# The last down-projection group as a product of seven, its products summed in PSUM banks, and the up projection's second half in blocks of 256 columns

## The chip, the cores and the metric

One core of one Trainium2 chip. The metric is the device time of one execution in microseconds (us). The engines are named as in the profile: PE (TensorE, matmul) and PEld (its weight loads), DVE (VectorE), ACT (ScalarE), POOL (GpSimd) and SP (SyncE, which here only issues DMAs). A letter q behind a name (SPq) is that engine's queue of issued DMAs and waits.

## The reference, cut to what matters

The block is one layer over 512 tokens of width 1024. Everything ahead of the MLP (a gated delta rule, a retention, an output projection and a norm) is left as it is. What the change touches is the end:

```python
hn = rmsnorm(x, n_mlp_pre)                       # x: 512 tokens x 1024
ff = jnp.square(jax.nn.relu(hn @ w_up)) @ w_down # w_up 1024 x 4096, w_down 4096 x 1024
return x + rmsnorm(ff, n_mlp_post)
```

Inputs and outputs are fp32. The kernel splits each fp32 operand into a high part (rounded to fp32r) and a low part (the rest), and makes three matmuls of each product: high by high, high by low, low by high.

## The kernel before

**Groups.** The MLP runs over four groups of 1024 columns of `w_up` (which are 1024 rows of `w_down`). Of each group the up projection comes first, then the down projection of the same 1024 features, which is added into `facc`, the 512 x 1024 sum over groups that stays in SBUF.

**Up projection.** `feature_major` makes the transposed product: for 512 columns (four blocks of 128 features, one PSUM bank of tag `mm` each) it loads four weight tiles of 256 rows x 512 columns; each serves 24 matmuls of 512 tokens. A group has two such halves. `Squares.take` empties a bank: ScalarE makes relu and square into `r`, then `split` makes the high part on ScalarE (a cast) and the low part on VectorE (a subtraction).

**Down projection of groups 0 to 2.** The 1024 features x 512 tokens and the 1024 x 1024 weights are cut into quarters, and seven products of quarters take the place of eight (the scheme of Strassen and Winograd). Each product is 2 x 4 x 3 = 24 matmuls of 128 x 128 by 512 columns, with two weight tiles. Three products use sums of quarters: `first_sums` and `other_sums` make those of the features on VectorE, and `BlockSums` those of the weights: a plain DMA copies a quarter into DRAM scratch (`copy`, line 169, SP's queue), and an accumulating DMA of GpSimd adds another to it (`add_block`, line 135, POOL's queue). Copies and adds are dropped into the stream of weight loads by `pace`, one job for each 8.5 us of planned time. The seven results are combined on ScalarE and VectorE through the SBUF tiles `p1` and `u2` into `facc`.

**Down projection of group 3.** It is made with all eight products, by `row_tiles`: eight weight tiles of 128 rows x 1024 columns are loaded, split and kept in SBUF. Row tiles 0 and 1 (a row tile is 128 tokens) are made together, then row tile 2, then 3; `ff_done` adds each to `facc`, norms it (`add_normed`: square sums on ScalarE, weighting by `wpost` on VectorE, a root with one Newton step, the sum with the residual `x2`), and two DMAs store it.

**Weight tiles.** Every weight tile is loaded into one of four `raw` buffers by SP's queue, in order; ScalarE casts it to the high part (line 148), VectorE subtracts to get the low part (line 149). The split halves go into rings of three (`whi`, `wlo`), or into a kept tile. A `raw` buffer comes free when VectorE has made the low part, and SP's next load waits for that.

**Order.** The order of the instructions on each engine is set by a scheduler at build time from priorities; each engine then works through its own queue strictly in that order.

Of the kernel before, what the change touches and what calls it, by code (L numbers as in the profile page):

```python
# [19 lines left out]
P = 128  # L20
# [43 lines left out]
def hybrid_block_kernel(ctx: ExitStack, tc: tile.TileContext, a: dict, out: bass.AP):  # L64
# [137 lines left out]
    ga_sums = BlockSums(w_in, OFF_GA, OFF_GA + 512, "ga", False)  # L202
    vg_sums = [BlockSums(w_in, OFF_VB + h * 512, OFF_GB + h * 512, f"vg{h}", False) for h in range(4)]
    gb_sums = BlockSums(w_in, OFF_GBR, OFF_GBR + 512, "gb", False)
    down_sums = [BlockSums(w_down[grp * D : (grp + 1) * D, :], 0, 512, f"dn{grp}") for grp in range(3)]
    for sums in [z_sums, ga_sums] + vg_sums + [gb_sums] + down_sums:
        later_adds.extend((*pair, sums) for pair in sums.adds())

# [91 lines left out]
        times(d, "s4", x, True)  # L300
        out(0, 1, d, p1, ALU.add)

    def token_product(quarters):

        pinned = []

        def product(pss, x, ks, wts, first):
            wh, wl = wts
            xh, xl = quarters[x]
            for t in range(2):  # L310
                tt = slice(t * P, (t + 1) * P)
                for kk in range(2):
                    k = 2 * ks + kk
                    lhs, rhs = (xh[:, k, tt], xl[:, k, tt]), (wh[:, kk, :], wl[:, kk, :])
                    tick(1536)
                    for i in range(3):
                        m = nc.tensor.matmul(  # L317
                            pss[t], lhs[i // 2], rhs[i % 2],
                            start=first and k + i == 0, stop=k + i == 5, skip_group_check=not first,
                        )  # L320
# [1353 lines left out]
    with tc.tile_pool(name="pm", bufs=1) as pm:  # L1674
# [49 lines left out]
            nc.vector.scalar_tensor_tensor(v[:, 1:2], ss[:, 1:2], 1.0 / D, v[:, 0:1], ALU.mult, ALU.add)  # L1724
            return root(v[:, 1:2])

        def add_normed(t, parts, w):

            fw = pm.tile([P, D], F32, tag="ym", name="fw", bufs=2)

            def weigh(half):
                nc.vector.tensor_tensor(fw[:, hss[half]], parts[half], w[:, hss[half]], ALU.mult)

            y = norm_halves([(p, weigh) for p in parts])
            for half in range(2):
                x = x2[:, t, hss[half]]
                nc.vector.scalar_tensor_tensor(x, fw[:, hss[half]], y, x, ALU.mult, ALU.add)
            return fw
# [50 lines left out]
        class Squares:  # L1789


            def __init__(self, grp):
                self.r = pm.tile([P, 2, 2, 4, 256], F32, tag="r4", name="r4")
                og = [act.tile([P, 2, 4, 256], F32R, tag="og", name="ffq") for _ in range(2)]
                a2 = act.tile([P, 2, 2, 4, 256], F32R, tag="actT", name="ffq")
                self.a2 = a2
                self.dst = {
                    "11": [og[0][:, 0], og[0][:, 1]],
                    "12": [a2[:, 0, 0], a2[:, 1, 0]],
                    "22": [a2[:, 0, 1], a2[:, 1, 1]],  # L1800
                }
                self.last = grp == 3
                if self.last:
                    self.dst["21"] = [og[1][:, 0], og[1][:, 1]]
                else:
                    s23 = act.tile([P, 2, 2, 4, 256], F32R, tag="actT", name="ffq")
                    s4 = pm.tile([P, 2, 4, 256], F32R, tag="s4", name="ffq")
                    for i, s in enumerate((og[1], s23[:, 0], s23[:, 1], s4)):
                        self.dst[f"s{i + 1}"] = [s[:, 0], s[:, 1]]

            def fs(self, name, f):
                return [w[:, f : f + 2, :] for w in self.dst[name]]
# [1 line left out]
            def take(self, kh, f, ps, th=None):  # L1814
# [4 lines left out]
                elif kh:  # L1819
                    square_relu(  # L1820
                        ps.rearrange("p (h t) -> p h t", h=2), r, [self.a2[:, i, :, f, :] for i in range(2)]
                    )
                else:
                    square_relu(ps.rearrange("p (h t) -> p h t", h=2), r, None)
                    for th in range(2):
                        name = f"{th + 1}1"
                        if name in self.dst:
                            split(r[:, th], [w[:, f, :] for w in self.dst[name]])

            def first_sums(self, f):  # L1830

# [4 lines left out]
                nc.vector.tensor_tensor(r11, r22, r11, ALU.subtract)  # L1836
                self.sums_mark = split(r11, self.fs("s2", f))[0]

            def other_sums(self):

                split(self.r[:, 1, 1], self.dst["s1"])
                split(self.r[:, 0, 1], self.dst["s3"])
                nc.vector.tensor_tensor(self.r[:, 1, 0], self.r[:, 1, 0], self.r[:, 0, 0], ALU.add)
                split(self.r[:, 1, 0], self.dst["s4"])

        def seven_down(grp, x):

            src = w_down[grp * D : (grp + 1) * D, :]
            plain, summed = block_products(src, down_sums[grp], token_product(x))
            p1, u2 = ([pm.tile([P, T], F32, tag="u", name=n, bufs=4) for _ in range(2)] for n in ("p1", "u2"))  # L1850

            def add(th, ch, parts, op=ALU.add, new=False):
                with tc.high_priority(400 if new else 0):
                    for t in range(2):
                        dst = facc[:, 2 * th + t, hss[ch]]
                        if new and not grp:
                            nc.scalar.copy(dst, parts[t])
                        else:
                            nc.vector.tensor_tensor(dst, dst, parts[t], op)
# [9 lines left out]
            plain(a, "12", 1, 0, False)  # L1869
            add(0, 0, a, new=True)  # L1870
            b = bank(psm)
            summed(b, "s2", 2, True)
            with tc.high_priority(400):
                for t in range(2):
                    nc.vector.tensor_tensor(u2[t], p1[t], b[t], ALU.add)
            c = bank(psx)
            summed(c, "s1", 1, True)
            add(1, 1, c, new=True)
            summed(b, "s3", 3, False)
            with tc.high_priority(400):  # L1880
                for t in range(2):
                    nc.vector.tensor_tensor(p1[t], p1[t], b[t], ALU.add)
            add(1, 1, p1, ALU.subtract)
            add(1, 0, p1)
            plain(c, "s4", 1, 512, False)
            add(0, 1, c, new=True)
            add(0, 1, u2, ALU.subtract)

        facc = pm.tile([P, 4, D], F32, tag="facc", name="facc")
        for grp in range(4):  # L1890
            sq = Squares(grp)
            for half in range(2):
                for th in (None,) if grp or half else (1, 0):
                    tt = slice(0, T) if th is None else slice(256 * th, 256 * th + 256)
                    pss = feature_major(w_up, [h[:, :, tt] for h in hn], grp * 1024 + half * 512, 512, 8)
                    for f in range(4):
                        with tc.high_priority(150 * half):
                            sq.take(half, f, pss[f], th)
                            if half and f % 2 and not sq.last:
                                sq.first_sums(f - 1)  # L1900
            if not sq.last:
                sq.other_sums()
            if grp < 3:
                seven_down(grp, sq.dst)
            else:
                wk = four_keeps(act, "actT") + s4_keep()
                for i in range(2):
                    h = pm.tile([P, 8, T], F32R, tag=f"hn{i}", name="keep").rearrange("p k t -> p (k t)")
                    wk += [(h[:, j * 1024 : j * 1024 + 1024], h[:, j * 1024 + 1024 : j * 1024 + 2048]) for j in (0, 2)]
                wk += four_keeps(pm, "r4")[:1]  # L1910

                def ff_tile(kt, t):
                    tt = slice((t % 2) * P, (t % 2 + 1) * P)
                    return [w[:, kt % 4, tt] for w in sq.dst[f"{t // 2 + 1}{kt // 4 + 1}"]]

                def ff_done(t, ps):
                    parts = [facc[:, t, hs] for hs in hss]
                    for half in range(2):
                        nc.vector.tensor_tensor(parts[half], parts[half], ps[half], ALU.add)
                    add_normed(t, parts, wpost)  # L1920
                    for half in range(2):
                        eng = nc.scalar if half else nc.sync
                        eng.dma_start(out[0, t * P : (t + 1) * P, hss[half]], x2[:, t, hss[half]])

                row_tiles(w_down, ff_tile, grp * 8, lambda kt: wk[kt], ff_done, ((0, 1), (2,), (3,)))


# [25 lines left out]
```

## Time and profile before

| | us |
|---|---|
| median of three runs (1340.27 to 1342.88) | 1341.09 |
| the profiled execution | 1340.97 |
| its span, first to last instruction | 1339.2 |
| PE busy in the span | 1323.0 (99%) |
| VectorE busy | 935.8 (70%) |
| ScalarE busy | 637.6 (48%) |
| mean granted clock of TensorE | 0.999 |

The span is from the first to the last instruction; the rest of the execution's time, 1340.97 - 1339.2 = 1.8 us, lies around it. Matmuls are pipelined: a matmul of 512 columns is recorded as 0.39 us, but the next one starts 0.23 us after it, so the busy time of PE does not tell how far PE is from its best; the distance between starts does. In the tables of groups a row reads: line, engine, operation, output <- inputs, shapes and count, then busy time, mean ns of one, and the idle time of the engine just before them with what ended it. In the timeline a row is start, duration, engine, line and operation, and in brackets how long the engine had waited and for whom. Where a row of the timeline merges several instructions (x3), its duration runs from the first one's start to the last one's end.

### The profile page before, as it was taken

Reading aid. Unit: us, or ns where it says so; the run is one execution under the profiler, and the core shown is the slowest. Engines: PE = TensorE matmul, PEld = TensorE weight load, DVE = VectorE, ACT = ScalarE, POOL = GpSimd, SP = SyncE. Lnnn points to the kernel's source line nnn. Section 1 sums busy time; section 2 is a strip of 40 time slices with the busy share of each in tenths; the row PEclk is TensorE's granted clock in tenths of the full one; section 3 lists DMA queues with packets and bytes.
Section 4 is the critical chain, followed back from the end, with each engine's and each line's share of the span. In section 5 each row is a group of like instructions: output and inputs, shape, how many; then the busy total and the mean of one; then the engine's idle time right before and its main releaser. Section 6 shows DMA issues by size and latency. Waiting matters only on the chain.

```text
span 1339.2 us, 17492 instructions
## 1 busy us (share of the span) xinstructions
PE 1323.0 (99%) x6615; PEld 1095.8 (82%) x6615; DVE 935.8 (70%) x1575; ACT 637.6 (48%) x1126; POOL 78.1 (6%) x83
## 2 busy tenths in 40 slices
PE   9999999999999999999999999999999999999997
PEld 7888888887788888888888888878888888888886
DVE  6889867485666577877577776889684755829535
ACT  5783436554534533553443443445264745346441
POOL 2101100000000000100010000000001010000000
PEclk9999999999999999999999999999999999999999
DMA  5336952567775665996394361535629893635421
GB/s 192 131 111 157 206 117 72 119 164 179 199 165 136 141 194 145 270 259 124 110 251 111 113 205 61 169 130 173 220 75 247 216 275 115 190 103 177 128 79 63
DMA packets 105701, 210.57 MB, mean 157 GB/s; under 512 B 6598, under 2 KB 30320, under 8 KB 105104
## 3 DMA queue, kind: packets, MB, share of 16 engines
q1 hardware_dynamic: 88592, 167.27, 39.0%
q0 software_dynamic: 14704, 35.30, 16.3%
q10 hardware_dynamic: 2320, 6.89, 1.4%
q8 instruction: 52, 0.85, 0.3%
q14 instruction: 33, 0.27, 0.1%
HBM read 205.21 MB, written 62.93 MB: 200 GB/s over the span
## 4 chain that ended last, share of the span: by engine, by line
PE 83%; DVE 7%; ACT 5%; DMA 4%; issue 1%; DVEq 0%; ACTq 0%; SPq 0%
PE mm L668 17%; PE mm L317 12%; PE mm L95 11%; PE mm L94 11%; PE mm L93 11%; PE dl L317 8%; PE dl L668 5%; DVE wlo L149 2%; DMA raw<-in_w_in_dram 2%; PE dl L93 1%; PE dl L95 1%; PE dl L94 1%; DMA raw<-sums 1%; PE tr L397 1%; PE tr L677 1%
## 5 line engine op out<-in xcount | busy, mean ns | idle before, releaser
L148 ACT CAST whi<-raw 128x1024 fp32r<-128x1024 f32 x259 | 272.0, 1052 | 414.3 <-PE mm L94 94.6
L149 DVE TENSOR_TENSOR wlo<-raw,whi 128x1024 fp32r<-128x1024 f32 x259 | 315.4, 1221 | 213.7 <-ACT whi L148 212.1
L668 PE MATMUL mm<-actT,whi 128*128 128x512 f32 x448 | 144.3, 403 | 0.0
L317 PE MATMUL mm<-whi,xsum 128*128 128x512 f32 x384 | 120.4, 390 | 0.0
L95 PE MATMUL mm<-hn,wlo 128*128 128x512 f32 (+1 forms) x288 | 105.4, 366 | 0.0
L94 PE MATMUL mm<-hn,whi 128*128 128x512 f32 (+1 forms) x288 | 105.3, 366 | 0.0
L93 PE MATMUL mm<-hn,whi 128*128 128x512 f32 (+1 forms) x288 | 105.3, 366 | 0.0
L668 PEld LDWEIGHTS mm<-actT,whi 128*128 128x128 f32 x448 | 80.5, 188 | 14.9
L668 PE MATMUL mm<-actT,wlo 128*128 128x512 f32 x224 | 87.8, 392 | 0.0
L317 PEld LDWEIGHTS mm<-whi,xsum 128*128 128x128 f32 x384 | 72.0, 188 | 14.8
L317 PE MATMUL mm<-wlo,xsum 128*128 128x512 f32 x192 | 75.1, 391 | 0.4 <-DVE wlo L149 0.4
L668 PE MATMUL mm<-whi,og 128*128 128x512 f32 x192 | 62.5, 397 | 0.0
L95 PEld LDWEIGHTS mm<-hn,wlo 128*128 128x128 f32 x288 | 54.3, 189 | 8.8
L94 PEld LDWEIGHTS mm<-hn,whi 128*128 128x128 f32 x288 | 54.3, 189 | 8.7
L93 PEld LDWEIGHTS mm<-hn,whi 128*128 128x128 f32 x288 | 54.3, 189 | 8.7
L668 PE MATMUL mm<-whi,actT 128*128 128x512 f32 x176 | 60.4, 405 | 1.0 <-DVE qf L906 1.0
L317 PE MATMUL dl<-whi,ffq 128*128 128x512 f32 x192 | 61.1, 389 | 0.0
L317 PE MATMUL dl<-whi,actT 128*128 128x512 f32 x192 | 61.0, 389 | 0.0
L1785 DVE TENSOR_TENSOR ffq<-r,ffq 128x512 fp32r<-128x512 f32 (+2 forms) x51 | 33.7, 676 | 29.1 <-ACT ffq L1785 29.0
L135 POOL DMA_DIRECT2D sums<-in_w_in_dram x28 | 32.6, 1163 | 365.3 <-DMA sums<-in_w_in_dram 365.3
L93 PE MATMUL mm<-actT,whi 128*128 128x512 f32 x128 | 51.5, 403 | 0.0
L95 PE MATMUL mm<-actT,wlo 128*128 128x512 f32 x128 | 50.8, 397 | 0.0
(394 smaller groups left out, 2885.9 us busy)
## 6 DMA issues: line engine op xcount, KB each, us to landing
raw<-in_w_in_dram SPq DMA_DIRECT2D x95, 512.0 KB, 4.8
raw<-sums SPq DMA_DIRECT2D x56, 512.0 KB, 4.1
raw<-in_w_up_dram SPq DMA_DIRECT2D x36, 512.0 KB, 5.3
sums<-in_w_in_dram SPq DMA_DIRECT2D x32, 512.0 KB, 5.5
sums<-in_w_in_dram POOLq DMA_DIRECT2D x28, 512.0 KB, 7.8
raw<-in_w_down_dram SPq DMA_DIRECT2D x26, 512.0 KB, 3.9
sums<-in_w_down_dram SPq DMA_DIRECT2D x24, 512.0 KB, 6.7
sums<-sums POOLq DMA_DIRECT2D x16, 512.0 KB, 7.9
```

What stands on the lines that cost most here:

```text
L93: nc.tensor.matmul(ps, lh, rh, start=first, stop=False)
L94: nc.tensor.matmul(ps, lh, rl, start=False, stop=False)
L95: nc.tensor.matmul(ps, ll, rh, start=False, stop=last)
L135: tc.keep_in_program_order(nc.gpsimd.dma_start(dst, src, accum_op=ALU.add))
L148: nc.scalar.copy(hi[:, :n], raw[:, :n])
L149: nc.vector.tensor_tensor(lo[:, :n], raw[:, :n], hi[:, :n], ALU.subtract)
L317: m = nc.tensor.matmul(pss[t], lhs[i // 2], rhs[i % 2], start=first and k + i == 0, stop=k + i == 5, skip_group_check=not first,)
L397: nc.tensor.transpose(ps, src, ident)
L668: m = tc.keep_in_program_order(nc.tensor.matmul(*args, **kwargs))
L677: tc.keep_in_program_order(nc.tensor.transpose(ps, src, ident if by is None else by))
L1785: return nc.scalar.copy(dst[0], r), nc.vector.tensor_tensor(dst[1], r, dst[0], ALU.subtract)
```

## The change

- The last group is made with seven products too; `down_sums` has a fourth set, so eight more copies and eight more accumulating adds of 512 KB go through the DMA queues.
- The seven results are no longer combined through `p1` and `u2`. Three pairs of PSUM banks (`a`, `b`, `c`) each take several products one after the other without being cleared, and after each product the running sum of a bank is added to or subtracted from the quarter of `facc` that needs it.
- The up projection's second half is made as two blocks of 256 columns, with weight tiles of 512 rows x 256 columns; each block's squares and sums are made as soon as it is there.
- In group 3, row tiles 0 and 1 are finished after five products. The last two products are made row tile by row tile (`token_product(x, (t,))`) with weights that are kept in SBUF: `s3` for row tiles 2 and 3, then `22` for 2 and 3. The class `Finish` takes the place of `ff_done` and norms a row tile half by half; all stores of row tiles 2 and 3 are ordered behind the last add.

```diff
-    down_sums = [BlockSums(w_down[grp * D : (grp + 1) * D, :], 0, 512, f"dn{grp}") for grp in range(3)]
+    down_sums = [BlockSums(w_down[grp * D : (grp + 1) * D, :], 0, 512, f"dn{grp}") for grp in range(4)]
...
-            fw = pm.tile([P, D], F32, tag="ym", name="fw", bufs=2)
+            fw = pm.tile([P, D], F32, tag="ym", name="fw", bufs=4)
...
-            def other_sums(self):
-
-                split(self.r[:, 1, 1], self.dst["s1"])
-                split(self.r[:, 0, 1], self.dst["s3"])
-                nc.vector.tensor_tensor(self.r[:, 1, 0], self.r[:, 1, 0], self.r[:, 0, 0], ALU.add)
-                split(self.r[:, 1, 0], self.dst["s4"])
+            def other_sums(self, f, last):
+
+                r, fs = self.r[:, :, :, f : f + 2, :], lambda name: self.fs(name, f)
+                for name in ("s1", "s4", "s3") if last else ("s1", "s3", "s4"):
+                    if name == "s4":
+                        nc.vector.tensor_tensor(r[:, 1, 0], r[:, 1, 0], r[:, 0, 0], ALU.add)
+                    split(r[:, int(name != "s3"), int(name != "s4")], fs(name))
...
+            a = bank(psx)
             plain(a, "11", 0, 0, True)
-            with tc.high_priority(400):
-                for t in range(2):
-                    nc.scalar.copy(p1[t], a[t])
-            d = bank(psm)
-            summed(d, "22", 4, True)
-            add(1, 0, d, new=True)
...
+            add(0, 0, a, new=True, prio=100)
+            b = bank(psm)
+            plain(b, "12", 1, 0, True)
+            add(0, 0, b, prio=0)
+            c = bank(psm)
+
+            def s1():
+                summed(c, "s1", 1, True)
+                add(1, 1, c, new=True)
+
+            def s2():
+                summed(a, "s2", 2, False)
+                add(0, 1, a, ALU.subtract, new=True)
+
+            def s3():
+                summed(a, "s3", 3, False)
+                add(1, 1, a, ALU.subtract)
+
+            for step in (s1, s2) if grp == 3 else (s2, s1, s3):
+                step()
+            plain(c, "s4", 1, 512, False)
+            add(0, 1, c, prio=0)
+            if grp < 3:
+                summed(a, "22", 4, False)
+                add(1, 0, a, new=True)
+                return
+            for t in range(2):
+                rows = Finish(t)
+                for half in range(2):
+                    rows.half(half)
+                for half in range(2):
+                    rows.store(half)
...
+            rows = [Finish(2 + t) for t in range(2)]
+            for name, half, op in (("s3", 1, ALU.subtract), ("22", 0, ALU.add)):
                 for t in range(2):
+                    for ks in range(2):
+                        token_product(x, (t,))(a, name, ks, ws[name, ks], False)
+                    dst = facc[:, 2 + t, hss[half]]
+                    with tc.high_priority(400):
+                        done = nc.vector.tensor_tensor(dst, dst, a[t], op)
+                    rows[t].half(half)
+            for r in rows:
+                for half in range(2):
+                    with tc.issue_after(done.ins):
+                        r.store(half)
...
+            for th in (None,) if grp else (1, 0):
+                tt = slice(0, T) if th is None else slice(256 * th, 256 * th + 256)
+                pss = feature_major(w_up, [h[:, :, tt] for h in hn], grp * 1024, 512, 8)
+                for f in range(4):
+                    sq.take(0, f, pss[f], th)
+            for f in (0, 2):
+                pss = feature_major(w_up, hn, grp * 1024 + 512 + f * P, 256, 8)
+                with tc.high_priority(150):
+                    for i in range(2):
+                        sq.take(1, f + i, pss[i])
+                    sq.first_sums(f)
+                sq.other_sums(f, grp == 3)
+            seven_down(grp, sq.dst)
```

Two places show what this does to the engines' queues. The first is the very end of VectorE's queue, from the second-last add into `facc` (before: row tile 3's first half; after: row tile 2's last half). `facc<-facc,mm` and `facc<-facc,dl` are adds of a PSUM bank, `fw` is the weighting by the norm's gains, `nh_v` and `nr` are the small steps of the norm's root, and `acc<-fw,nr_y,acc` is the final sum that the store waits for. Before:

```order
L1919 TENSOR_TENSOR facc<-facc,mm 128x512
L1732 TENSOR_TENSOR fw<-facc,post 128x512
L1723 TENSOR_SCALAR nh_v<-nh_s 128x1
L1919 TENSOR_TENSOR facc<-facc,mm 128x512
L1732 TENSOR_TENSOR fw<-facc,post 128x512
L1724 SCALAR_TENSOR_TENSOR nh_v<-nh_s,nh_v 128x1
L412 RECIPROCAL nr_y<-nr_y 128x1
L414 SCALAR_TENSOR_TENSOR nr_t<-nr_y 128x1
L415 TENSOR_TENSOR nr_t<-nr_t,nh_v 128x1
L416 SCALAR_TENSOR_TENSOR nr_y<-nr_t,nr_y 128x1
L1737 SCALAR_TENSOR_TENSOR acc<-fw,nr_y,acc 128x512 x2
```

The same end now, from the last add on (the rows ahead of it are the add of row tile 2 and the start of its root):

```order
L1904 TENSOR_TENSOR facc<-facc,dl 128x512
L414 SCALAR_TENSOR_TENSOR nr_t<-nr_y 128x1
L1924 TENSOR_TENSOR fw<-facc,post 128x512
L415 TENSOR_TENSOR nr_t<-nr_t,nh_v 128x1
L1926 SCALAR_TENSOR_TENSOR nh_v<-nh_s,nh_v 128x1
L416 SCALAR_TENSOR_TENSOR nr_y<-nr_t,nr_y 128x1
L1934 SCALAR_TENSOR_TENSOR acc<-fw,nr_y,acc 128x512
L412 RECIPROCAL nr_y<-nr_y 128x1
L1934 SCALAR_TENSOR_TENSOR acc<-fw,nr_y,acc 128x512
```

Behind these rows stand row tile 3's three small steps and its two final sums. So between the last add and row tile 3's final sums stand now, beside row tile 3's own steps, three small steps and both final sums of row tile 2, which before had been through long before.

The second place is SP's queue from the last group's up projection to the end. Before, from the middle of group 2's products on:

```order
L103 DMA raw<-in_w_down_dram 128x2x512 x2
L197 DMA raw<-sums 128x1024 x6
L103 DMA raw<-in_w_down_dram 128x2x512 x2
L103 DMA raw<-in_w_up_dram 128x2x512 x8
L103 DMA raw<-in_w_down_dram 128x1024 x8
L1923 DMA out_dram<-acc 128x512 x4
```

After, with the last copy of a weight quarter for this group in the first row:

```order
L169 DMA sums<-in_w_down_dram 128x2x512
L103 DMA raw<-in_w_up_dram 128x2x512 x4
L103 DMA raw<-in_w_up_dram 128x4x256 x4
L103 DMA raw<-in_w_down_dram 128x2x512 x4
L197 DMA raw<-sums 128x1024 x4
L103 DMA raw<-in_w_down_dram 128x2x512 x2
L197 DMA raw<-sums 128x1024 x4
L1936 DMA out_dram<-acc 128x512 x4
```

The last group now takes fourteen weight tiles for its down projection instead of eight, eight of them from the sums that GpSimd makes, and the eight copies for these sums stand in SP's queue among the weight loads of groups 1 and 2 (the last of them is the first row here).

More of the change, by code (lines that the diff above doesn't have):

```diff
@@ L1801, in __init__ @@
                 }
[L1802 to L1809, printed above, removed]
+                s23 = act.tile([P, 2, 2, 4, 256], F32R, tag="actT", name="ffq")
+                s4 = pm.tile([P, 2, 4, 256], F32R, tag="s4", name="ffq")
+                for i, s in enumerate((og[1], s23[:, 0], s23[:, 1], s4)):
+                    self.dst[f"s{i + 1}"] = [s[:, 0], s[:, 1]]
             def fs(self, name, f):
@@ L1869, in seven_down @@
[L1869 to L1882, printed above, removed]
@@ L1891, in hybrid_block_kernel @@
             sq = Squares(grp)
[L1892 to L1925, printed above, removed]
```

59 lines of the change are left out of this document (41 added, 18 removed).

## The prediction

> **What bounds the kernel now.** The page's busy times and its chain of waits come first.
>
> ```profile
> PE 1323.0 (99%) x6615; PEld 1095.8 (82%) x6615; DVE 935.8 (70%) x1575; ACT 637.6 (48%) x1126; POOL 78.1 (6%) x83
> PE 83%; DVE 7%; ACT 5%; DMA 4%; issue 1%; DVEq 0%; ACTq 0%; SPq 0%
> ```
>
> PE sets the time. Since a busy PE is not PE at its peak, I read the chain for the last 140 us next, for the distance of the matmuls, and the waits of PEld in the MLP (PE itself has none there):
>
> ```profile
> 1206.29 5.44 PE dl L317 x24
> 1211.72 5.44 PE mm L317 x24
> ...
> 1238.92 5.44 PE dl L317 x24
> ...
> 1288.11 0.41 PE mm L94
> ...
> 1331.44 0.24 PE mm L95
> 1331.70 0.70 DVE facc L1919
> PEld mm L94 <- DVE keep L149: 0.3, 1, 0.3
> PEld dl L317 <- DVE wlo L149: 0.3, 1, 0.3
> PEld mm L93 <- ACT r L1780: 0.2, 1, 0.2
> ```
>
> A product of 24 matmuls takes 5.44 us, 0.227 us each, with the next one right behind it; from 1040 us to the last matmul PEld waits 0.8 us in all. So there is no stall left to win in the MLP: only fewer matmuls, or a shorter tail behind the last of them, can make it faster. The tail is this:
>
> ```profile
> 1331.70 0.69 DVE L1919 TENSOR_TENSOR facc<-facc,mm 128x512 f32<-128x512 f32 x1 [3.75 <-PE mm L95]
> 1332.42 0.69 DVE L1732 TENSOR_TENSOR fw<-facc,post 128x512 f32<-128x512 f32 x1
> 1333.24 0.16 DVE L1724 SCALAR_TENSOR_TENSOR nh_v<-nh_s,nh_v 128x1 f32<-128x1 f32 x1
> 1333.67 0.17 DVE L412 RECIPROCAL nr_y<-nr_y 128x1 f32<-128x1 f32 x1 [0.27 <-ACT nr_y L411]
> 1334.26 0.16 DVE L416 SCALAR_TENSOR_TENSOR nr_y<-nr_t,nr_y 128x1 f32<-128x1 f32 x1
> 1334.45 1.42 DVE L1737 SCALAR_TENSOR_TENSOR acc<-fw,nr_y,acc 128x512 f32<-128x512 f32 x2
> 1335.90 0.34 ACTq L1923 DMA_DIRECT2D out_dram<-acc  x1
> ```
>
> The last matmul ends at 1331.44 + 0.24 = 1331.68, VectorE adds at once (it had waited 3.75 us), and its last sum ends at 1334.45 + 1.42 = 1335.87: 4.2 us. The last store and the end take 1339.2 - 1335.9 = 3.3 us more.
>
> **The matmuls removed.** The last group's eight products become seven: 192 matmuls become 168, at the same shape of 128 x 128 by 512. 24 x 0.227 = **-5.44 us**, all of it on the path, if PE stays as dense.
>
> **Up projection in blocks, sums in PSUM: 0.** A weight tile of 512 x 256 serves 2 blocks x 4 x 3 = 24 matmuls, as one of 256 x 512 does, so PE's work is the same; its rows of 1 KB could land later. The first weight loads of the kernel have that shape:
>
> ```profile
> raw<-in_w_in_dram SPq DMA_DIRECT2D x7, 512.0 KB, 4.6
> raw<-in_w_up_dram SPq DMA_DIRECT2D x8, 512.0 KB, 7.9
> raw<-in_w_down_dram SPq DMA_DIRECT2D x8, 512.0 KB, 3.7
> ```
>
> The first row (20 to 70 us) has 4.6 us to landing in tiles of 256 columns; the second is the 512-column form from 1060 to 1110 us, the third from 1255 to 1300. In the up projection a tile lasts 5.44 us and four `raw` buffers are in turn, so even 7.9 us is covered. If that cover went, each us beyond four tiles' time would be a us of PE. The products' new order leaves each bank one product, 5.44 us, between its end and its next use, as `a` had before; in that time two adds of 0.6 us must come. Groups 1 and 2 lose four VectorE adds (18 to 14) and two ScalarE copies each, which nobody waited for: 0.
>
> **Eight more copies and adds: 0, at a bound.** They are paced behind group 2's, so they fill groups 1 and 2, where the DMA engines have room:
>
> ```profile
> 1000.00:1110.00 110.00, 109.71 (x565) 93.95 (x564) 63.35 (x79) 61.95 (x98) 12.00 (x12) 1.00 0.92 238
> 1110.00:1206.00 96.00, 96.00 (x425) 79.49 (x424) 54.02 (x64) 45.94 (x62) 0.00 (x0) 1.00 0.43 137
> 1206.00:1289.00 83.00, 83.00 (x367) 68.50 (x366) 52.77 (x65) 41.42 (x58) 0.00 (x0) 1.00 0.42 134
> 1230.54 21.78 SPq L103 DMA_DIRECT2D raw<-in_w_up_dram  x8
> sums<-in_w_down_dram SPq DMA_DIRECT2D x6, 512.0 KB, 7.9
> sums<-in_w_down_dram POOLq DMA_DIRECT2D x6, 512.0 KB, 13.1
> ```
>
> (The last two numbers are the DMA share and GB/s; PE's busy time is the third.) From 1000 to 1110 us the same kind of jobs ran at a share of 0.92 and PE lost 0.3 us; the next 180 us stand at 0.43. Sixteen jobs more at 8.5 us each make about 136 us of what 1000 to 1110 already is. The last copy stands in SP's queue just ahead of the last group's up weights, which are issued at 1230.5 us: 7.9 us for the copy and 13.1 for the add give 1252, and the first such sum is loaded for a product that begins at 1288 + 10.9 us.
>
> **The new tail: +2.2 us, the term that I had to choose.** VectorE had been half idle in the last group (23.2 us busy in 42.7, from the first row here); now it has a group's sums, twelve weight tiles and four norms in 38.1 us of matmuls. The distance of its instructions in a full queue comes from rows of group 2 and of row tile 0:
>
> ```profile
> 1289.00:1331.70 42.70, 42.66 (x188) 34.86 (x187) 23.16 (x48) 13.69 (x30) 0.00 (x0) 1.00 0.22 75
> 1241.40 1.89 DVE L1859 TENSOR_TENSOR facc<-facc,p 128x512 f32<-128x512 f32 x3
> 1220.10 2.35 DVE L149 TENSOR_TENSOR wlo<-raw,whi 128x1024 fp32r<-128x1024 f32 x2
> 1310.39 0.15 DVE L1723 TENSOR_SCALAR nh_v<-nh_s 128x1 f32<-128x1 f32 x1
> 1310.46 0.67 DVE L1919 TENSOR_TENSOR facc<-facc,mm 128x512 f32<-128x512 f32 x1
> 1206.34 0.69 DVE L1785 TENSOR_TENSOR ffq<-r,ffq 128x512 fp32r<-128x512 f32 x1 [1.46 <-ACT ffq L1785]
> ```
>
> Three adds of 512 end 1.89 us after the first starts, with 0.68 for the last: 0.60 from start to start. Two weight tiles in 2.35 us: 1.14. The two final sums in 1.42: 0.67 each. A small step lets the next start after 0.07 us if that is independent; in the tail above, where each waits for the last, 0.19; I take 0.13. From the end of the last up matmul, VectorE's queue has 12 weight tiles (13.7 us), 9 sums and halves of features, 14 adds into `facc` and 8 weightings (31 x 0.60 = 18.6), 8 final sums (5.3) and 24 small steps (3.1): **40.7 us**. Ahead of the last add stand 35.5 of these. To that come its waits: before the first sums for ScalarE's squares and casts (1.46 in the row above, at the same place of group 2, and some 0.5 for the second feature block), some 0.1 at each of a dozen dependent pairs, and 0.4 for the kept weights' last landing; I estimate 3.5 us. So it reaches the last add at 39.1, when PE ended at 38.1: **1.0 us late**. From the add to the last sum it needs the 4.2 us of before, and row tile 2's two final sums and three small steps (1.33 + 0.4), of which its 0.5 us of idle time between the rows from 1332.42 to 1333.67 hides some: +1.2. Tail 1.0 + 4.2 + 1.2 = 6.4 us: +2.2.
>
> Its bounds: with no lateness and half of the 1.2 hidden, +0.6. With every instruction at its own recorded duration instead of its distance (31 x 0.69, 12 x 1.22, 8 x 0.71, 24 x 0.16: 45.5 us), 4.8 us more: +7.0. I take the low side, since group 2's rows are this kind of queue.
>
> [...]
>
> **Sum.** 1340.97 - 5.44 + 2.2 = **1337.7 us** for an execution like the profiled one, which lies 0.1 us under the median of 1341.09.
>
> **Rivals.** A *slow queue*: VectorE takes the recorded durations; it reaches the last add some 5.8 us late, partly by making PE wait for a bank or low parts. 1340.97 - 5.44 + 7.0 = 1342.5. For it: these are the durations that the trace records. Against it: the distances above, and group 2, where between the gap at 1206.34 and the next one VectorE ran 25 us on end while PE did not wait:
>
> ```profile
> 1231.93 1.22 DVE L149 TENSOR_TENSOR wlo<-raw,whi 128x1024 fp32r<-128x1024 f32 x1 [0.28 <-ACT whi L148]
> ```
>
> A *short tail*: the norms of row tiles 0 to 2 fall into VectorE's gaps, +0.6: 1336.1. For it: 40.7 us of queue is barely over PE's 38.1. Against it: the order of its queue is fixed, so a late row holds all behind it.
>
> *Late weights* (slower): the copies and adds now run beside the products of groups 1 and 2, which take a tile in 2.72 us. Four buffers cover 4 x 2.72 = 10.9 us from issue to use, and from there each us is one of PE.
>
> ```profile
> DMA to landing us min/median/max: 4.1/7.4/16.2
> ```
>
> From 1000 to 1060 us, under the jobs of groups 1 and 2, the latest tile took 16.2 us: 5.3 us too long if it hit a product. Two such hits make 10.6: 1348.3; it decides from 6.1 us on (1343.8). For it: the same jobs will stand beside twice as many products. Against it: PE lost 0.3 us in all of 1000 to 1110, with a median of 7.4 us to landing.
>
> **Chances.** The forecast 0.57, the short tail 0.12, the slow queue 0.18, late weights 0.13. A measurement of this kernel can tell about 0.2% (2.7 us) from no change: faster is below 1338.4, slower above 1343.8. The forecast's own range is 1336.3 to 1339.3, with about 0.86 of its chance below 1338.4: 0.49. Faster 0.49 + 0.12 = 0.61, within 0.2% 0.08 + 0.18 = 0.26, slower 0.13. The range goes from just under the short tail, 1335.8, to 1342.0, most of the slow queue.
>
> **What would show it.** The last up matmul where it was, near 1288; seven products of 5.44 us behind it, the last ending near 1326.2; VectorE without a gap of note in the last 30 us; its last add about 1 us behind the last matmul and its last sum about 6.4; no new waits of PEld. Wrong would be: PE waiting for `wlo`, `keep` or an add of `facc` in the last group (then the queue is slower than I took it), or matmuls of groups 1 and 2 further apart than 0.227 us (late weights).

## The result, and the profile after

| | before | the change |
|---|---|---|
| median of nine runs (us) | 1341.16 (1338.09 to 1342.88) | **1335.0** (1333.11 to 1337.96) |
| the profiled execution | 1340.97 | 1335.0 |
| its span | 1339.2 | 1333.2 |
| first matmul of the first down-projection product, at | 1042.7 | 1040.8 |
| from there to the end of the span | 296.5 | 292.4 |

The ratio is 0.996, with a 95% interval of 0.995 to 0.9971. The forecast was 1337.7, and the lower end of its range 1335.8.

The page of the change shows the engines' busy times and the chain by engine in the same places as before:

```profile
PE 1317.0 (99%) x6591; PEld 1091.5 (82%) x6591; DVE 949.4 (71%) x1599; ACT 650.7 (49%) x1139; POOL 86.2 (6%) x91
...
PE 83%; DVE 7%; ACT 5%; DMA 4%; issue 2%; DVEq 0%; ACTq 0%
```

PE still sets the time. It has 24 matmul records less, VectorE 24 instructions more, GpSimd the eight adds more. The chain of waits has the same distance for a product of 24 matmuls as before, here in groups 0, 1 and 2 (in the last group it runs through VectorE, so that group is read from PE's rows below):

```profile
1040.96 5.44 PE dl L317 x24
...
1123.63 5.44 PE dl L317 x24
...
1205.23 5.44 PE dl L317 x24
...
1237.87 5.44 PE dl L317 x24
```

PE's waits from 940 us to 1340 us are one for a late weight tile's low part, some 30 us into group 0's products, and one ahead of the MLP:

```profile
PE mm L317 <- DVE wlo L149: 0.8, 1, 0.8
PE tr L397 <- DVE fw L1763: 0.3, 1, 0.3
```

Two stretches of the table of busy time show the last group's seven products, and then the tail (columns as before: length, then PE, PEld, DVE, ACT, POOL, the clock, the DMA share, GB/s):

```profile
1286.80:1324.90 38.10, 38.10 (x169) 31.21 (x167) 36.09 (x61) 21.79 (x36) 0.00 (x0) 1.00 0.43 140
1324.90:1330.30 5.40, 0.01 (x1) 0.00 (x0) 5.05 (x15) 0.99 (x4) 0.00 (x0) 0.90 0.26 97
```

VectorE's share of the last group went from 23.16 us in 42.7 to 36.09 us in 38.1, and PE is busy through all of it. From its first matmul's start to its last one's end the last group's down projection took 1331.68 - 1287.72 = 43.96 us before, and takes 1324.91 - 1286.67 = 38.24 now: 5.7 less. The end itself is read in the timeline, PE's last row first:

```profile
1323.16 1.75 PE L317 MATMUL dl<-keep,ffq 128*128 128x512 f32 x7
```

VectorE's rows, from a full stretch of its queue and from the end:

```profile
1300.82 1.87 DVE L1851 TENSOR_TENSOR facc<-facc,mm 128x512 f32<-128x512 f32 x3
...
1323.03 0.68 DVE L1904 TENSOR_TENSOR facc<-facc,dl 128x512 f32<-128x512 f32 x1
...
1324.99 0.16 DVE L412 RECIPROCAL nr_y<-nr_y 128x1 f32<-128x1 f32 x1 [0.27 <-ACT nr_y L411]
1325.07 0.67 DVE L1904 TENSOR_TENSOR facc<-facc,dl 128x512 f32<-128x512 f32 x1
...
1326.86 0.75 DVE L1934 SCALAR_TENSOR_TENSOR acc<-fw,nr_y,acc 128x512 f32<-128x512 f32 x1
...
1327.60 0.73 DVE L1934 SCALAR_TENSOR_TENSOR acc<-fw,nr_y,acc 128x512 f32<-128x512 f32 x1
...
1328.83 1.41 DVE L1934 SCALAR_TENSOR_TENSOR acc<-fw,nr_y,acc 128x512 f32<-128x512 f32 x2
```

The last matmul ends at 1323.16 + 1.75 = 1324.91. The last add starts at 1325.07, 0.16 us later (before, 0.02). It is row tile 3's; row tile 2's, at 1323.03, stood 2.04 us ahead of it, and of the steps between them one (the reciprocal at 1324.99) waited for ScalarE. Between the last add and the last two sums stand row tile 2's two sums, one each at 1326.86 and 1327.60. The last sum ends at 1328.83 + 1.41 = 1330.24, so 5.17 us after the last add began, where it was 4.17 before. From there to the end of the span it is 1333.2 - 1330.24 = 2.97 us, where it was 3.33. Behind the last matmul everything together takes 8.3 us instead of 7.5: the new tail costs **0.8 us, not 2.2**.

The table shows a second piece that the forecast did not have: the MLP's down-projection products began 1.9 us earlier. Of what lies ahead of them only group 0's up projection is changed, and it takes the same time: from its first matmul to the first product 47.4 us in both (995.3 to 1042.7, and 993.4 to 1040.8). What the earlier start is worth is the subject of some of the runs below.

### The profile page after: what moved, and what is told of

It reads as the page before. It is cut to its first block, busy times and chain, and to the rows that moved or that the text cites. A ratio compares the mean times of both kernels' runs of the same rounds, so it can differ in the third digit from the quotient of the medians.

```text
span 1333.2 us, 17536 instructions
## 1 busy us (share of the span) xinstructions
PE 1317.0 (99%) x6591; PEld 1091.5 (82%) x6591; DVE 949.4 (71%) x1599; ACT 650.7 (49%) x1139; POOL 86.2 (6%) x91
## 4 chain that ended last, share of the span: by engine, by line
PE 83%; DVE 7%; ACT 5%; DMA 4%; issue 2%; DVEq 0%; ACTq 0%
PE mm L668 17%; PE mm L317 14%; PE mm L94 10%; PE mm L93 10%; PE mm L95 10%; PE dl L317 9%; PE dl L668 5%; DVE wlo L149 2%; DMA raw<-sums 2%; PE dl L93 1%; PE dl L95 1%; PE dl L94 1%; PE tr L397 1%; PE tr L677 1%; ACT whi L148 1%
## 5 line engine op out<-in xcount | busy, mean ns | idle before, releaser
L148 ACT CAST whi<-raw 128x1024 fp32r<-128x1024 f32 x269 | 282.8, 1053 | 406.6 <-PE mm L317 84.1
L149 DVE TENSOR_TENSOR wlo<-raw,whi 128x1024 fp32r<-128x1024 f32 x269 | 328.1, 1222 | 211.8 <-ACT whi L148 210.6
L668 PE MATMUL mm<-actT,wlo 128*128 128x512 f32 x224 | 87.8, 392 | 0.0
L317 PE MATMUL dl<-whi,ffq 128*128 128x512 f32 x224 | 71.3, 389 | 0.0
L317 PE MATMUL mm<-whi,ffq 128*128 128x512 f32 x192 | 61.0, 389 | 0.0
L1786 DVE TENSOR_TENSOR ffq<-r,ffq 128x512 fp32r<-128x512 f32 (+1 forms) x64 | 39.1, 621 | 27.0 <-ACT ffq L1786 26.9
```

Of the source, the lines that this page charges most:

```text
L148: nc.scalar.copy(hi[:, :n], raw[:, :n])
L149: nc.vector.tensor_tensor(lo[:, :n], raw[:, :n], hi[:, :n], ALU.subtract)
L317: m = nc.tensor.matmul(pss[t], lhs[i // 2], rhs[i % 2], start=first and k + i == 0, stop=k + i == 5, skip_group_check=not first,)
L668: m = tc.keep_in_program_order(nc.tensor.matmul(*args, **kwargs))
L1786: return nc.scalar.copy(dst[0], r), nc.vector.tensor_tensor(dst[1], r, dst[0], ALU.subtract)
```

## The experiments

All times in us. Where a ratio is given, it is to the kernel before, run on the same chip in the same series, with its 95% interval; the kernel before had medians of 1341.16 there (the change), 1339.98 (`scratch_only`, `old_last`, `no_jobs`, `eight`) and 1341.00 (`after_again`, `pool_fw`, `up_whole`). Three of the rows have one execution only, the profiled one.

| run | median (runs) | ratio to before | first product at | from there to the end | lost in group 0 |
|---|---|---|---|---|---|
| before, first profile | 1341.16 (9) | 1 | 1042.7 | 296.5 | 0.2 |
| `before_again` | 1343.88 (1) | | 1045.2 | 296.9 | 0.7 |
| `scratch_only` | 1340.70 (12) | 1.0002 [0.9992, 1.0011] | 1041.6 | 297.2 | 0.9 |
| `old_last` | 1340.05 (11) | 1.0002 [0.9992, 1.0011] | 1042.3 | 297.6 | 1.3 |
| the change | 1335.00 (9) | 0.996 [0.995, 0.9971] | 1040.8 | 292.4 | 1.1 |
| `after_again` | 1336.93 (11) | 0.9972 [0.996, 0.9984] | 1038.9 | 292.5 | 1.2 |
| `no_jobs` | 1337.22 (9) | 0.9972 [0.9959, 0.9985] | 1039.4 | 292.2 | 0.4 |
| `no_row2` | 1333.96 (1) | | 1040.3 | 291.9 | 1.6 |
| `weigh_twice` | 1336.84 (1) | | 1042.3 | 292.7 | 0.5 |
| `eight` | 1341.16 (12) | 1.0005 [0.9993, 1.0016] | 1043.2 | 297.5 | 1.3 |
| `pool_fw` | 1340.00 (12) | 0.9989 [0.998, 0.9997] | 1039.9 | 297.4 | 2.2 |
| `up_whole` | 1343.26 (10) | 1.0016 [1.0004, 1.0028] | 1041.1 | 300.5 | 2.0 |

The last three columns are of each run's profiled execution. The last one is what the 168 matmuls of group 0's down projection take from the first one's start to the next up projection, beyond 168 x 0.2267 us. Most of it is one wait for a late low part of a weight tile, as in the row of the change's waits above. It is part of the column before it, and it scatters between runs with the same code there (0.2 to 0.9 with the old code), so differences of a few tenths are read without it.

**The scratch alone.** The change takes four more DRAM tiles, which move those allocated after them. This kernel is the one before with four unused tiles:

```diff
+    spare = [dr.tile([P, 4, 512], F32, tag=f"dn3{i}", name="sums", bufs=1) for i in (2, 1, 3, 0)]
```

> The kernel before, with a fourth set of four DRAM scratch tiles set aside and never used. The profiled run of the change was already 1.9 us early when the MLP began, ahead of any edited instruction. If the place of tensors in DRAM does this, this kernel is 1 to 2 us faster than the one before and its first down-projection product starts near 1041 us (before: 1042.9). If that was the scatter of single executions, it is within 0.7 us of the kernel before in the median.

The ratio is 1.0002: where the scratch lies changes nothing that can be measured. Its first product did start early, at 1041.6 as expected of a kernel that gains by this, but the next two runs show that one start says little.

**The change and the kernel before, again.** Both unaltered, for the scatter of what lies ahead of the MLP.

> The change once more, unaltered, to part what it does from the scatter of single executions. From the first down-projection product to the end the profiles show 296.5 us before and 292.4 after (4.1 less, 4.9 without a wait of PE in group 0 that also came in a kernel without the edits); the start of that product has moved between 1039.4 and 1043.2 us in six kernels whose work ahead of it is the same. Theory 'the change is worth what the MLP shows': 4 to 5 us under the kernel before, ratio 0.9963 to 0.997, and 292 to 292.5 us from the first product to the end again. Rival 'the work ahead of the MLP became faster too': ratio 0.9955 or less, and the first product starts below 1041 us again.

> The kernel before once more, for the scatter of single executions: from the first down-projection product to the end 296.4 to 297.3 us again. If the work ahead of the MLP is the same in both kernels, its first product may start anywhere between 1039 and 1043 us; if the change makes that work faster, at 1041.5 or later again.

The view of one line's instructions gives the first product of each; first the change again:

```profile
L317 PE MATMUL dl<-whi,ffq x32: 389/389/389, 1038.9 to 1055.0; 128*128 128x512 f32 x32
```

and the kernel before again:

```profile
L317 PE MATMUL dl<-whi,ffq x28: 389/389/389, 1045.2 to 1059.9; 128*128 128x512 f32 x28
```

The same code as in the first profiles began 2.5 us later in the one case and 1.9 us earlier in the other. Over all twelve executions, with the same work ahead but for the blocks of group 0's up projection, the products began between 1038.9 and 1045.2. From there to the end, the pairs agree with themselves: 296.5, 296.9 (and 297.2 in `scratch_only`) against 292.4 and 292.5. So the change in the MLP is **-4.4 us** by the means 296.9 and 292.45; without what is lost in group 0 it is -4.9 (296.2 or 296.3 in all three against 291.3 in both). The two ratios of whole executions give -5.4 (0.4% of 1341) and -3.8 (0.28%), on either side of it; the second, 0.9972, lies just outside the band that I expected.

The rival's other sign came in both runs (starts below 1041 and above 1041.5), so I looked for the place where the starts part. In all twelve executions PE, VectorE and SP work through the same instructions in the same order up to 970 us, and the largest part of the scatter arises between 325 and 370 us, some 600 us ahead of any edited instruction. The 150 matmuls from the 2001st on take 34.0 to 38.2 us there; from their end to the first product it is 678.4 to 679.9 us in all twelve. PE's busy time in this stretch, in the kernel before again and in the change again, and the waits of the former (the latter has none):

```profile
325.00:370.00 45.00, 42.40 (x182) 33.26 (x180) 22.92 (x31) 23.52 (x45) 2.27 (x2) 1.00 0.69 189
325.00:370.00 45.00, 44.99 (x200) 37.32 (x200) 25.97 (x35) 25.89 (x51) 3.40 (x3) 1.00 0.76 204
PE dl L668 <- ACT vt L1309: 1.4, 2, 1.0
PE mm L668 <- DVE wlo L149: 0.8, 1, 0.8
PE dl L668 <- DVE st L1323: 0.3, 1, 0.3
```

So the early start is not work of the changed part. Why these operands are later in one execution than in another was not tried, and whether the edits can move them from afar stays open: the three starts with the old MLP are 1041.6 to 1045.2, the nine with any edit 1038.9 to 1043.2, and these overlap. Open is also whether the change itself adds some of the loss in group 0.

**The last group with eight products, the rest changed.** Only the last group's down projection goes back to the old code; the sums in PSUM stay in groups 0 to 2, and the blocks of 256 columns in all four.

```diff
-    down_sums = [... for grp in range(4)]
+    down_sums = [... for grp in range(3)]
...
+            if grp < 3:
+                seven_down(grp, sq.dst)
+                continue
...
+            row_tiles(w_down, ff_tile, grp * 8, lambda kt: wk[kt], ff_done, ((0, 1), (2,), (3,)))
```

> The new up-projection blocks and the sums in PSUM in groups 0 to 2, but the last group with eight products, stores and tail as before. Theory 'only the matmuls count': within 0.7 us of the kernel before. Rival 'blocks and PSUM sums win something too' (less VectorE work, fewer waits): 1 to 2.5 us faster than before, and then the last group alone won less than its 5.44 us.

The ratio is 1.0002, and 297.6 less the 1.3 lost in group 0 is 296.3, as before. The PSUM sums and the blocks bring nothing by themselves and cost nothing; the gain is all in the last group's down projection.

**The matmuls given back.** The change, with one product of the last group (`s4`) multiplied twice: 24 matmuls more, and no load, split or add more. Its output holds that product twice.

```diff
+            plain, summed = block_products(src, down_sums[grp], token_product(x, twice=("s4",) if grp == 3 else ()))
...
+                    for i in [0, 1, 2] * (2 if x in twice else 1):
```

> The change with the last group's product s4 multiplied twice from the same weights (24 matmuls more, no load, split or add more; the output is not the reference's). If matmuls set the time and VectorE's queue is not late, it is 5.4 us slower than the change. If VectorE's queue is what ends last in the last group (a lateness of 1 us or more), part of the 5.4 is hidden: 3 to 4.5 us slower.

Without the loss in group 0 it is 296.2 against 291.3: the 24 matmuls give back 4.9 us, between the two bands that I expected. Ahead of the last matmul's end (1330.96 + 1.98 = 1332.94) they take 5.4 us, and the tail behind it is 0.5 shorter, 7.8 instead of 8.3. In VectorE's timeline its add for row tile 2 now waits for PE, and the last add is not late:

```profile
1330.25 0.69 DVE L1904 TENSOR_TENSOR facc<-facc,dl 128x512 f32<-128x512 f32 x1 [0.18 <-PE dl L317]
...
1332.97 0.69 DVE L1904 TENSOR_TENSOR facc<-facc,dl 128x512 f32<-128x512 f32 x1
```

**No copies and adds for the last group.** The sums of weight quarters are replaced by plain quarters, loaded from `w_down`, so the products get weights that are not the sums; the eight copies and eight adds are gone. (A group has four such sums, of two weight tiles each: `s1`, `s2`, `s3` and `22` use them, and `s1` to `s4` use sums of features. That makes five of the seven products, where the text on the kernel before has three.)

```diff
-    down_sums = [... for grp in range(4)]
+    down_sums = [... for grp in range(3)]
...
+    down_sums.append(Unsummed(w_down[3 * D : 4 * D, :]))
```

> The change without the eight copies and eight adds for the last group: its summed weight quarters are replaced by plain ones, so the output is not the reference's. Theory 'the jobs are hidden' (the prediction): same as the change to 0.7 us. Rival 'they cost': the 0.9 us by which group 0's products came later in the change, or more, is won back; 1 to 3 us faster than the change.

292.2 against 292.4; without the loss in group 0 it is 291.8 against 291.3. The copies and adds cost nothing behind group 0, and of group 0's loss at most the 0.7 us by which the two differ. The 0.5 us by which this run is longer lie in its tail of 8.75 us: its last add starts 0.60 us behind the last matmul. In `after_again` it is 0.04, so this distance alone moves by half a us between kernels with the same queue of VectorE. In the change itself, GpSimd issues the last of its adds 60 us before the first product that needs a sum:

```profile
1237.65 1.14 POOL L135 DMA_DIRECT2D sums<-in_w_down_dram  x1 [9.63 <-DMA sums<-in_w_down_dram]
```

**Up projection's second half in one piece.** The change with blocks of 512 columns again; squares and sums are then made of all four blocks after the whole half.

```diff
+            pss = feature_major(w_up, hn, grp * 1024 + 512, 512, 8)
             for f in (0, 2):
-                pss = feature_major(w_up, hn, grp * 1024 + 512 + f * P, 256, 8)
...
-                        sq.take(1, f + i, pss[i])
+                        sq.take(1, f + i, pss[f + i])
```

> The change with the up projection's second half in one piece of 512 columns again. Theory 'the blocks cost nothing and win nothing' (the prediction): same as the change to 0.7 us, no wait of PE. Rival 'the blocks make room for the sums': all four features' sums then come behind the end of the up projection, and in the last group, where s1 is already the third product, PE waits 2 to 5 us for them; groups 1 and 2, with a product more ahead, wait little.

1343.26, slower than before (1.0016), and 300.5 us for the MLP: 8.1 more than the change. PE's waits from 1010 us on, with the low parts of the feature sums (`ffq`) as a new cause:

```profile
PE mm L317 <- DVE ffq L1786: 3.0, 4, 1.5
PE dl L317 <- DVE ffq L1786: 1.5, 3, 0.5
PE dl L317 <- DVE wlo L149: 0.8, 1, 0.8
```

These 4.5 us for `ffq` are the recorded part; PE's weight loads waited 8.0 us for it. By the distances of PE's matmuls from start to start, beyond 0.2267 us each, groups 1 to 3 lose 6.2 us, half of it in the last group, where the change loses nothing. Another 0.9 is lost in group 0, and the tail is 0.7 longer: the last add starts 0.34 us behind the last matmul, and one more final sum stands behind it. So the blocks are worth nothing by themselves, as `old_last` shows, but without them the sums of features come late, in groups 1 and 2 too (1.5 us each), and the new ending does not pay.

**VectorE's load in the last group, more of it.** Row tiles 0 and 1 are weighted twice, four instructions of 512 more, about 2.4 us in the queue.

```diff
+                if self.t < 2:
+                    nc.vector.tensor_tensor(self.fw[:, hs], f, wpost[:, hs], ALU.mult)
```

> The change with the four weightings of row tiles 0 and 1 made twice on VectorE (the same values, the output is the reference's): four more instructions of 0.6 us, 2.4 us in VectorE's queue of the last group. Theory 'VectorE's queue of the last group is just full': its last add, 0.2 us behind the last matmul in the change, falls 1.5 us or more behind, or PE waits in the last two products, and from the first down-projection product to the end it takes 1.5 to 2.5 us more than the change's 292.4. Rival 'VectorE has 2 us to spare there': 292.4 to 292.9 us again.

292.7, or 0.9 us more than the change when both are taken without the loss in group 0 (292.2 against 291.3). In the last 38 us of matmuls VectorE is busy a little longer, and PE waits nowhere:

```profile
1287.80:1325.90 38.10, 38.08 (x169) 31.19 (x167) 36.79 (x63) 21.76 (x35) 0.00 (x0) 1.00 0.38 126
```

The end shows where the rest went:

```profile
1326.21 0.68 DVE L1904 TENSOR_TENSOR facc<-facc,dl 128x512 f32<-128x512 f32 x1
1326.81 0.74 DVE L1936 SCALAR_TENSOR_TENSOR acc<-fw,nr_y,acc 128x512 f32<-128x512 f32 x1
...
1329.23 2.73 DVE L1936 SCALAR_TENSOR_TENSOR acc<-fw,nr_y,acc 128x512 f32<-128x512 f32 x4
```

The last matmul ends at 1325.89, and the last add starts 0.3 us after it instead of 0.16, which is within the 0.04 to 0.60 of the runs above. VectorE's gaps in the stretch shrink from 2.0 to 1.3 us, and one of row tile 1's final sums now stands behind the last add: from there to the last sum's end it takes 5.75 us instead of 5.17, most of the 0.9. Of 2.4 us, about 1.5 found room. The 292.7 taken raw lies in the rival's band of 292.4 to 292.9; without the loss in group 0, a third of the load did cost time. So neither holds as written: the queue had some room, not enough for all of it. It is a single run.

**Row tile 2's final sums left out.** The change without them; what is stored for row tile 2 is the residual alone.

```diff
+                if self.t != 2:
+                    nc.vector.scalar_tensor_tensor(x, self.fw[:, hss[half]], self.y, x, ALU.mult, ALU.add)
-                nc.vector.scalar_tensor_tensor(x, self.fw[:, hss[half]], self.y, x, ALU.mult, ALU.add)
```

> The change without row tile 2's two final sums on VectorE (its rows are stored without the MLP's result, so the output is not the reference's). Theory 'the longer tail is row tile 2's sums standing ahead of row tile 3's': the time from the last add's start to the last sum's end falls from 5.2 us to 4.2. Rival 'VectorE is late because of the whole queue of the last group': it falls by 0.3 us or less, and the last add starts as far behind the last matmul as before.

VectorE's timeline at the end:

```profile
1325.08 0.67 DVE L1904 TENSOR_TENSOR facc<-facc,dl 128x512 f32<-128x512 f32 x1
...
1327.03 0.16 DVE L412 RECIPROCAL nr_y<-nr_y 128x1 f32<-128x1 f32 x1 [0.20 <-ACT nr_y L411]
...
1327.81 1.41 DVE L1935 SCALAR_TENSOR_TENSOR acc<-fw,nr_y,acc 128x512 f32<-128x512 f32 x2
```

From the last add to the last sum's end it takes 1329.22 - 1325.08 = 4.14 us, as before the change (4.17), and the whole MLP without the loss in group 0 is 1.0 shorter, 290.3 against 291.3: the 1.0 us that the change has more in its tail are these two sums. They hide some 0.3 us of their 1.3, since the norm now waits 0.20 us for ScalarE again.

**Weightings on GpSimd.** An attempt to go faster than the change, by taking eight instructions off VectorE.

```diff
-                nc.vector.tensor_tensor(self.fw[:, hs], f, wpost[:, hs], ALU.mult)
+                nc.gpsimd.tensor_tensor(self.fw[:, hs], f, wpost[:, hs], ALU.mult)
```

> The change with the eight weightings (fw) of the last norm on GpSimd instead of VectorE: 8 x 0.6 us less in VectorE's queue, and row tile 2's final sums then stand behind the last add, where VectorE waits for ScalarE. If the tail is VectorE's queue, the time from the last matmul to the last sum falls by 0.5 to 1.0 us. If GpSimd takes over 2 us for one weighting, or slows VectorE, it is the same or up to 2 us longer.

297.4 us, 5 more than the change, 1.1 of it in group 0; by the medians of one series it is 3.1 more (1340.00 against 1336.93). Either is worse than the 2 us that I expected at most. Three of GpSimd's rows, and VectorE's rows beside them:

```profile
1320.80 1.74 POOL L1924 TENSOR_TENSOR fw<-facc,post 128x512 f32<-128x512 f32 x1 [1.95 <-DVE facc L1904]
1324.41 2.98 POOL L1924 TENSOR_TENSOR fw<-facc,post 128x512 f32<-128x512 f32 x2 [1.87 <-DVE facc L1904]
1329.10 1.70 POOL L1924 TENSOR_TENSOR fw<-facc,post 128x512 f32<-128x512 f32 x1 [1.71 <-DVE facc L1904]
```

```profile
1321.64 0.91 DVE L414 SCALAR_TENSOR_TENSOR nr_t<-nr_y 128x1 f32<-128x1 f32 x1
...
1325.25 0.68 DVE L1904 TENSOR_TENSOR facc<-facc,dl 128x512 f32<-128x512 f32 x1
...
1328.94 2.41 DVE L1934 SCALAR_TENSOR_TENSOR acc<-fw,nr_y,acc 128x512 f32<-128x512 f32 x2
```

The last weighting takes 1.70 us there, against 0.69 on VectorE, and VectorE's instructions beside them get longer: two final sums take 2.41 us instead of 1.41, a small step 0.91 instead of 0.15. That step ends at 1321.64 + 0.91 = 1322.55, when GpSimd's ends (1320.80 + 1.74 = 1322.54), so it looks held until then rather than slowed. Not all are: the add at 1325.25, which takes one operand from PSUM, has its usual 0.68, though GpSimd is at work from 1324.41 to 1327.39. Which operands decide was not tried, and by what VectorE is held no run shows. PE's waits there, for banks that VectorE has not added yet, come to 1.7 us.

## Why the prediction was off, by its steps

**The matmuls, -5.44: right.** Products stand 5.44 us apart as before, and `eight` gives 5.4 us back ahead of the last matmul's end. The old last group stood a little wider than 192 x 0.2267 us, so 5.7 went; with the tail's +0.8 this makes the -4.9 that the MLP shows.

**Blocks and sums in PSUM, 0: the sum right, the cover incomplete.** I named only the landing of the weights as what the blocks could touch. `up_whole` shows that the blocks also give VectorE and ScalarE the time for the feature sums; without them the MLP is 8.1 us longer.

**Copies and adds, 0: right.** `no_jobs` has the same MLP within 0.5 us on either reading, and the *late weights* did not come: no wait of PE in groups 1 to 3.

**The tail, +2.2: mis-sized; measured +0.8.** This is the step of the sum that failed. It has three parts.

- *VectorE reaches the last add 1.0 us late*: 0.16 measured, and 0.04 in `after_again`. The distances I took were right: a row of three adds still takes 1.87 us, and 512-column instructions start 0.60 apart. The work was counted a little low: by the order of the queue eight small steps stand behind the last add, so 35.9 us stand ahead of it, not 35.5. What was too high are the 3.5 us of waits, most of which I had estimated without a row. In the 38.10 us VectorE is busy 36.09, so that its gaps are 2.0; with the 0.16 behind the last matmul that makes the 38.3 at which it came to the add, where I had 39.1. I read this as independent work standing next in the queue behind most dependent pairs; no run took that apart. The lateness does not add up to the end either: at row tile 2's last add VectorE is 0.8 us behind PE, but from there to the last add it needs 2.04 us and PE 2.72. An independent instruction starts 0.08 us after a small step, as behind the reciprocal ahead of the last add (1324.99 to 1325.07); I had taken 0.13 as the mean of both kinds.
- *Row tile 2's two sums and small steps, +1.2*: +1.0, shown by `no_row2`.
- *The final store and the end, 3.3 as before*: 2.97. I had carried it over unchanged; without this shortening, whose cause was not tried, the tail would cost 1.1.

Of the rivals, the *short tail* (+0.6, 1336.1) is the nearest; the *slow queue* is out, since PE waited for nothing in the last group and its own sign, a wait for a bank, did not show. The recorded durations by which it counts hold for one add alone (0.69 us, `eight` at 1330.25), and not for an add's share of a full queue: three adds in 1.87 us here too (1300.82).

**The base of the sum, and the range: a term was missing.** With +0.8 in place of +2.2 the sum would be 1340.97 - 5.44 + 0.8 = 1336.3, where the profiled execution of the change took 1335.0. Most of the rest lies ahead of the MLP: 1.9 us from the earlier start, of which group 0 takes 0.9 back (0.2 lost before, 1.1 now). The wider spacing of the old last group gives the other 0.3. Since the start of the products varied by 6.3 us over twelve executions, and the median of the very same kernel was 1335.0 in one series and 1336.9 in the next (outside the range and inside it), a range whose lower end lay 0.3 us under the shortest forecast was too narrow below: it had bounds for the change's own terms, and none for the scatter of the execution from which the sum was made. The gain that belongs to the change is 4.4 to 4.9 us where 3.2 was forecast; that part is off by the tail.

## What to carry to other kernels

Where work moves onto an engine that then runs nearly full beside the bounding one, count its queue by the distance of instructions from start to start (0.60 us here for 512 columns, where one add alone is recorded with 0.69), and add only such waits as a row shows: an estimate of waits is the first thing to bound (2.0 us here where 3.5 were put). A change that pays at the end of a kernel can depend on one that brings nothing alone: the blocks are neutral with the old ending, and worth 6 to 8 us with the new one (8.1 by the profiles, 0.9 of it in group 0, and 6.3 by the medians of one series). And before a difference of a few us is read from two profiled executions, look at where the changed part begins in each; measure from there, and give the range a term for what scatters ahead of it.

## What was not expected of the hardware

- With the same instructions up to 970 us, the first down-projection product began between 1038.9 and 1045.2 us, a scatter of 0.5%. Two thirds of it arise between 325 and 370 us, where PE waits 2.5 us for operands in one execution and not at all in another. Why they come late was not tried; the place of DRAM scratch changes nothing (1.0002).
- From the last sum's end to the end of the span it is 3.3 us in the four profiles with the old ending (before, `before_again`, `scratch_only`, `old_last`), and 3.0 in all eight with the new. The stores are of the same size (256 KB each, and 2.0 us from issue to landing before and in the change); the cause was not tried.
- GpSimd at work on 128 x 512 fp32 rows lengthened some of VectorE's: a step on 128 x 1 from 0.15 to 0.91 us, ending 0.01 us after GpSimd's instruction, and two final sums from 1.41 to 2.41, but not an add from PSUM (0.68).
